# Twelve pairs of column tiles of a second block's input projection by seven block products, with the recurrence's gates and output gates laid out anew

## Chip, core and metric
One NeuronCore of one Trainium2 chip runs the whole program. The time is the device time of an execution in microseconds (us), as the median of three runs. The engines are TensorE (PE, matmuls; its weight loads are PEld), VectorE (DVE), ScalarE (ACT), GpSimd (POOL) and SyncE (SP), whose queue issues the DMAs.

## What is computed
Two transformer blocks, float32, 1024 tokens of width 1024. Block 1 is a windowed attention and a SwiGLU feed-forward; it is touched only in that its feed-forward calls a function now that held its text before. Block 2 begins with a mixer, and its input projection is what changes:

```python
proj = h @ w_in          # h: 1024 x 1024, w_in: 1024 x 5832
(q_m, k_m, v_m, o_m, i_m, f_m, c_q, c_kv, k_r, gate_pre) = jnp.split(proj, IN_SPLIT_POINTS, axis=-1)
qk = jax.nn.silu(causal_depthwise_conv(jnp.concatenate([q_m, k_m], axis=-1), conv_w, conv_b))
...
y_m = mlstm_chunkwise(q_m, k_m, v_m, log_i, log_f).reshape(B, S, M_V_WIDTH)
y_m = jax.nn.sigmoid(o_m) * y_m
...
merged = g_m * (y_m @ w_branch_m) + g_a * (y_a @ w_branch_a)
```

The widths are 1024 for q_m and k_m together, 1024 for v_m, 1024 for o_m (output gates), 4 and 4 for i_m and f_m (the recurrence's gates), 384 for c_q (query latents), 256 and 64 for c_kv and k_r (key latents), 2048 for gate_pre (gates of the merge).

## The kernel before
**Precision.** Each operand of a large product is split into a high part in a shorter float format (written by ScalarE) and a low rest (written by VectorE, high subtracted from the source). `split` does it, and `mm3` and `product` issue three matmuls for each block: high by high, low by high, high by low. `TH` and `TL` hold the split activations, transposed: 8 slices of 128 channels by 1024 tokens.

**Two forms of a projection.** `col_rows` makes a column tile: 128 output columns are the stationary weights and 512 tokens move, so a tile takes two halves of 8 x 3 = 24 matmuls, 48 in all; the result lies transposed (channels by tokens). `token_rows` makes 128 tokens by up to 512 columns: the activations are stationary and the weight columns move.

**Seven products.** The feed-forward of block 1 makes pairs of column tiles by a scheme with 7 block products in place of 8 (Strassen in Winograd's form): `block_sums` writes sums of the quarters of the activations (in place over a quarter of `TH` and `TL`, and into buffers), `left_sums` sums of the weights, which go to region 1 (`SP`). A pair takes 7 x 12 = 84 matmuls. The first pair is made in the usual way (`usual_first`, `usual_second`), because the sums are not there yet. `pair` makes the other pairs while `prep` prepares the weights of the next one.

**Order in block 2.** After the last pass of block 1 the norm of the second token half ends; meanwhile the first halves of three convolution tiles and of the recurrence's gates run on TensorE. `half_to_T` transposes the second half. Then: eight tiles of q_m and k_m (`conv`), each followed at once by its convolution on VectorE (four steps, lines 960 and 963) and a SiLU, stored in `qkd`; query latents and key latents by tokens; v_m and o_m by tokens (line 1034 onwards), o_m with the sigmoid, both stored by tokens; then the recurrence (`mlstm`, eight chunks of three steps), between whose steps the 16 tiles of the merge's gates are made as other work for TensorE; then `branch_m`, which loads the recurrence's output by tokens and transposes it into `TH` and `TL`.

**What sets the order.** The kernel is written on a tile framework. For each engine it draws up a list of instructions when the program is built: an instruction that is ready by its plan goes first if it stands earlier in the program, and one whose buffer or operand isn't ready is passed over. So the order on an engine isn't that of the source, but is fixed in the program. Buffers come from pools with a fixed number of slots per tag: `k4` 8, `vx` 4, `h2` 8, `k2` 4, `raw`, `wh`, `wl` 3 each; PSUM has three `mm`, three `s` and two `tp` banks. The big regions R1 to R3 are passed on whole: R1 is `Y`, then `SP` or `PU` (weights), then `ML` (recurrence), then `RC`.

Of the kernel before, what the change touches and what calls it, by code (L numbers as in the profile page):

```python
# [35 lines left out]
class Kernel:  # L36
# [554 lines left out]
    def block_sums(self, B):  # L591
# [23 lines left out]
        for k in range(4):  # L615
# [5 lines left out]
            nc.scalar.activation(x00, p00, AF.Identity, bias=B0)  # L621
            V.scalar_tensor_tensor(t1, p01, B0, x00, op0=OP.add, op1=OP.subtract)
# [49 lines left out]
    def block1_ffn(self, dbg=None):  # L672
# [39 lines left out]
        def first_two(j):  # L712

            A, T = self.left_parts(W[j]), self.T
            TT[j] = t = {}
            ps = self.pany()
            self.product(ps, A["a11"], T["00"])
            t[0] = self.h2([128, 512], "p1")
            nc.scalar.activation(t[0], ps, AF.Copy)
            yield  # L720
            ps = self.pany()
            self.product(ps, A["a12"], T["10"])
            t[2] = self.h2([128, 512], "sa")
            V.tensor_tensor(t[2], ps, t[0], op=OP.add)
            nc.scalar.activation(t[2], t[2], AF.Silu)

        def out(j, half, m):
            s = slice(half * 512, half * 512 + 512)
            h, l = self.h2([128, 512], "mh", F32R), self.h2([128, 512], "ml", F32R)
            self.split(h, l, m)  # L730
            for d, t in zip(midd, (h, l)):
                nc.sync.dma_start(d[j, :, s], f32(t))

        def pair(j, early):
# [21 lines left out]
            V.tensor_tensor(t[0], t[0], t[2], op=OP.mult)  # L756
            out(j, 0, t[0])
            yield
            add(t[1], t[1], "s4", "11")
            nc.scalar.activation(t[1], t[1], AF.Silu)  # L760
            V.tensor_tensor(t[3], t[3], t[1], op=OP.mult)
            out(j, 1, t[3])
            del W[j], TT[j]

# [9 lines left out]
        kept = []  # L774

        def usual_first():
            for n, A in enumerate(parts):
                ps = self.pany()
                self.product(ps, A["a11"], self.T["00"])
                p = self.h2([128, 512], "p1")  # L780
                nc.scalar.activation(p, ps, AF.Copy)
# [3 lines left out]
                t = self.h2([128, 512], "c1")  # L785
                V.tensor_tensor(t, ps, p, op=OP.add)
                kept.extend((p, t))
                if n == 0:
                    nc.scalar.activation(t, t, AF.Silu)
                    yield  # L790
            V.tensor_tensor(t, t, kept[1], op=OP.mult)
            out(0, 0, t)

        def usual_second():
            for A, p in zip(parts, (kept[0], kept[2])):
# [4 lines left out]
                if p is kept[0]:  # L800
                    nc.scalar.activation(p, p, AF.Silu)
            V.tensor_tensor(p, p, kept[0], op=OP.mult)
            out(0, 1, p)
# [7 lines left out]
        for k, _ in enumerate(self.block_sums(B2)):  # L811
            next(f, None)
        usual_second()
        SP = self.region(1, "SP", F32R)
        for _ in prep(1, True):
            pass
        cc2 = self.silu_col(a["c_2"], "cc2")
        mods = self.all_mods(("ada", self.cc, (("G2", 5, (0.0, "ffn_norm_post")),), 3, True),
                             ("mod", cc2, (("A3", 1, (1.0, "norm1_g_2")), ("B3", 0, None), ("Gm", 2, None),
                                           ("A4", 4, (1.0, "norm2_g_2"))), 3, True))  # L820
        for j in range(1, NH):
            nxt = prep(j + 1, False) if j + 1 < NH else iter(())
            for n, _ in enumerate(pair(j, j == 1)):
                next(nxt, None)
                if j > 1 and n in (0, 2, 4):
                    next(mods, None)
            for _ in nxt:
                pass
        for _ in mods:
            pass  # L830
        mods = self.all_mods(("mod", cc2, (("B4", 3, None), ("Ge", 5, None)), 3))
# [78 lines left out]
        for _ in norms:  # L910
            pass
        self.qkd = self.dram.tile([8, 128, S], F32, name="qkd")
# [33 lines left out]
    def conv(self, m):  # L946
# [3 lines left out]
        u = self.wunit(self.wcols("w_in_2", m * 128, 128), (8, 128))  # L950
        x = (self.k4 if m == 2 else self.vx)([128, S], "cx")
        for half in range(2):
            s = slice(half * 512, half * 512 + 512)
            ps = self.pany()
            self.col_rows(ps, half, u)
            nc.scalar.activation(x[:, s], ps, AF.Copy)
            if half == 0:
                yield
        o = self.k4([128, S], "co")
# [8 lines left out]
    def gates(self):  # L968

        nc, a = self.nc, self.a  # L970
        raw = self.h2([128, 8, 36], "gw")
        nc.gpsimd.memset(raw, 0.0)
        nc.sync.dma_start(raw[:, :, 0:4], self.wcols("w_in_2", 3072, 4))
        nc.sync.dma_start(raw[:, :, 32:36], self.wcols("w_in_2", 3076, 4))
        gh, gl = self.h2([128, 8, 36], "gwh", F32R), self.h2([128, 8, 36], "gwl", F32R)
        self.split(gh, gl, raw)
        gb = self.const.tile([36, 1], F32, name="gbias")
        nc.sync.dma_start(gb[0:4, :], a["igate_b_2"].rearrange("o h -> h o"))
# [10 lines left out]
    def block2_proj(self):  # L989
# [8 lines left out]
        for m in range(3, 8):  # L998
            for _ in self.convs[m]:
                pass  # L1000
# [982 lines left out]
```

## Time and profile before

| | us |
|---|---|
| median of 3 runs (lowest, highest) | 2809.21 (2807.45, 2810.56) |
| the profiled execution | 2807.71 |
| its span, first to last instruction | 2805.8 |
| TensorE busy in the span | 2627.1 |
| VectorE busy | 1765.9 |
| ScalarE busy | 1249.7 |

The mean granted clock of TensorE over the span is 0.976 of full speed. A busy TensorE is not one at its peak, because matmuls overlap; how many of them start in a stretch tells more. The change touches the stretch from 1190 to 1776 us of the span. A line like L724 is a line of the kernel's source; "out<-in" gives the tiles that an instruction writes and reads, and a note in brackets tells how long its engine was idle before it and what ended that.

### The profile page before, as it was taken

The page shows a single profiled execution, that of the slowest core. Times are in us where ns is not written, and L with a number is a line of the kernel's source. Part 1 is how long each engine was busy: PE and PEld are TensorE (multiplying, and loading weights), DVE is VectorE, ACT ScalarE, POOL GpSimd, SP SyncE. Part 2 cuts the span into 40 slices and gives each one's busy share as a digit, 9 for nine tenths or more (in the row PEclk, how much of TensorE's full clock was granted, in tenths as well). Part 3 has the DMA queues.
Part 4 walks back from the last instruction along what each step waited for, and adds up shares of the span by engine and source line. Part 5 has one row for each costly group of instructions (what it writes and reads, how often), then busy time and mean ns, then how long its engine had stood idle before and what let it go on. Part 6 is the DMA issues. An engine that isn't in the chain of part 4 may idle for free. (4 is left out here: it accounts for less than half of the span.)

```text
span 2805.8 us, 36372 instructions
## 1 busy us (share of the span) xinstructions
PE 2627.1 (94%) x13158; PEld 2116.6 (75%) x13158; DVE 1765.9 (63%) x3663; ACT 1249.7 (45%) x2183; POOL 219.3 (8%) x204
## 2 busy tenths in 40 slices
PE   6999998999999999899999999999999998889992
PEld 4766676788888787679888888788887887777771
DVE  6666549988887432866310444547777478788885
ACT  4666645333333210234222333435556444677772
POOL 0000002000000000200000000000000200343320
PEclk9999999999999999999999999999999999899996
DMA  7233113455555962534334565450111454799995
GB/s 245 91 98 98 37 75 120 130 167 168 172 170 164 292 190 83 171 104 147 118 109 128 177 172 170 152 180 14 31 31 61 152 196 164 247 341 322 314 325 177
DMA packets 316747, 442.11 MB, mean 158 GB/s; under 512 B 41633, under 2 KB 213726, under 8 KB 316566
## 3 DMA queue, kind: packets, MB, share of 16 engines
q1 hardware_dynamic: 307350, 422.97, 45.6%
q0 software_dynamic: 9216, 16.81, 2.5%
q8 instruction: 104, 1.70, 0.2%
q14 instruction: 77, 0.63, 0.1%
HBM read 354.39 MB, written 102.06 MB: 163 GB/s over the span
## 5 line engine op out<-in xcount | busy, mean ns | idle before, releaser
L164 DVE TENSOR_TENSOR wl<-raw,wh 128x1024 fp32r<-128x1024 f32 (+2 forms) x107 | 132.9, 1242 | 243.7 <-ACT wh L163 233.0
L163 ACT ACTIVATE wh<-raw 128x1024 fp32r<-128x1024 f32 (+2 forms) x107 | 111.5, 1043 | 238.2 <-PE mm L220 142.1
L164 DVE TENSOR_TENSOR mgl<-X,MH 128x1024 fp32r<-128x1024 f32 x91 | 110.0, 1221 | 16.5 <-ACT MH L163 16.0
L221 PE MATMUL mm<-TH,wl 128*128 128x512 f32 x288 | 114.6, 398 | 0.0
L219 PE MATMUL mm<-TH,wh 128*128 128x512 f32 x288 | 114.5, 397 | 0.0
L220 PE MATMUL mm<-TL,wh 128*128 128x512 f32 x288 | 114.2, 396 | 0.0
L1785 PEld LDWEIGHTS pss<-mgl,xh 128*128 128x128 f32 x512 | 96.4, 189 | 22.3
L163 ACT ACTIVATE MH<-X 128x1024 fp32r<-128x1024 f32 x91 | 96.3, 1062 | 37.8 <-DMA X<-in_w_expert_up_dram 15.9
L252 DVE SCALAR_TENSOR_TENSOR acc<-raw,cc,acc 128x1024 f32<-128x1024 f32 x70 | 89.8, 1283 | 30.9 <-DMA raw<-in_mod_w_dram 28.9
L219 PE MATMUL pss<-TH,wh 128*128 128x512 f32 x240 | 97.8, 408 | 5.7 <-ACT TH L163 4.4
L1785 PE MATMUL pss<-mgl,xh 128*128 128x256 f32 x512 | 102.9, 282 | 0.0
L1783 PE MATMUL pss<-MH,xh 128*128 128x512 f32 x256 | 102.7, 401 | 0.0
L1786 PE MATMUL pss<-MH,xl 128*128 128x512 f32 x256 | 101.6, 397 | 0.0
L442 DVE CUSTOM_DVE_ANT_0 pp<-pss,bias 128x384 f32<-128x384 f32 (+1 forms) x128 | 63.4, 521 | 54.4 <-PE pss L438 53.5
L220 PE MATMUL pss<-TL,wh 128*128 128x512 f32 x240 | 96.6, 403 | 0.0
L221 PE MATMUL pss<-TH,wl 128*128 128x512 f32 x240 | 96.3, 401 | 0.0
L551 POOL TENSOR_TENSOR Y<-Y,G 128x1024 f32<-128x1024 f32 x16 | 39.4, 2463 | 705.5 <-ACT junk L159 700.4
L228 PE MATMUL mm<-TH,wh 128*128 128x512 f32 x192 | 78.5, 410 | 1.0 <-ACT TH L350 1.0
L449 ACT ACTIVATE pp<-pp,mx 128x384 f32<-128x384 f32 (+1 forms) x128 | 73.8, 579 | 11.6 <-DVE mx L445 11.6
L229 PE MATMUL mm<-TL,wh 128*128 128x512 f32 x192 | 77.6, 404 | 0.0
L230 PE MATMUL mm<-TH,wl 128*128 128x512 f32 x192 | 76.6, 399 | 0.0
L219 PE MATMUL mm<-WD,mTh 128*128 128x512 f32 x128 | 55.6, 435 | 22.3 <-ACT mTh L163 22.3
(744 smaller groups left out, 8127.0 us busy)
## 6 DMA issues: line engine op xcount, KB each, us to landing
raw<-in_mod_w_dram SPq DMA_DIRECT2D x48, 512.0 KB
X<-in_w_expert_gate_dram SPq DMA_DIRECT2D x47, 512.0 KB
X<-in_w_expert_down_dram SPq DMA_DIRECT2D x47, 512.0 KB
raw<-in_ffn_w_in_dram SPq DMA_DIRECT2D x45, 512.0 KB
X<-in_w_expert_up_dram SPq DMA_DIRECT2D x44, 512.0 KB
raw<-in_w_in_dram SPq DMA_DIRECT2D x40, 512.0 KB
raw<-in_ada_w_dram SPq DMA_DIRECT2D x32, 512.0 KB
midh<-mh SPq DMA_DIRECT2D x44, 256.0 KB
```

Of the source, the lines that this page charges most:

```text
L163: self.nc.scalar.activation(h, src, AF.Copy)
L164: (engine or self.nc.vector).tensor_tensor(l, src, f32(h), op=OP.subtract)
L219: nc.tensor.matmul(ps, ah, bh, start=i == 0, stop=False)
L220: nc.tensor.matmul(ps, ah, bl, start=False, stop=False)
L221: nc.tensor.matmul(ps, al, bh, start=False, stop=i == n - 1)
L228: nc.tensor.matmul(ps, ah, bh, start=i == 0, stop=False)
L229: nc.tensor.matmul(ps, ah, bl, start=False, stop=False)
L230: nc.tensor.matmul(ps, al, bh, start=False, stop=i == n - 1)
L252: nc.vector.scalar_tensor_tensor(acc, raw, cc[:, k:k + 1], acc, op0=OP.mult, op1=OP.add)
L1783: nc.tensor.matmul(ps, xh[:, k], gh, start=k == 0, stop=False)
L1785: nc.tensor.matmul(ps[:, c], xh[:, k], self.ML[n + c][:, m], start=False, stop=False)
L1786: nc.tensor.matmul(ps, xl[:, k], gh, start=False, stop=k == 7)
```

## The change
The scheme of seven products becomes a function, `seven`, that the feed-forward of block 1 and now the projection of block 2 call. In block 2 it makes 24 column tiles, in 12 pairs: the 8 of q_m and k_m, the 8 of o_m and the last 8 of the merge's gates. The results are stored as they are (`qkr`, `og`, `gd`). Since the sums overwrite a quarter of `TH` and `TL`, `block_sums` also writes that quarter unsplit (`x01`) and stores it, and it is loaded and split again after the last pair.

After the pairs come the key latents by tokens, with the eight columns of the recurrence's gates beside them (356 columns with zeros between); the gates are transposed after each tile. Then the eight convolutions, whose input is loaded from `qkr`; then v_m by tokens. The query latents move into the recurrence as work between its first eight steps, and the first eight tiles of the merge's gates stay between the other sixteen. In `mlstm` the output gates are no longer loaded and multiplied; ScalarE scales the output. In `branch_m` each transposed group of 512 tokens is multiplied by the sigmoid of the loaded output gate before it is split.

```diff
-    def block_sums(self, B):
+    def block_sums(self, B, kept=None):
...
             nc.scalar.activation(x00, p00, AF.Identity, bias=B0)
+            if kept is not None:
+                x01 = self.k2([128, 512], "x01")
+                nc.scalar.activation(x01, p01, AF.Identity, bias=B0)
+                nc.sync.dma_start(kept[k], x01)
...
+    def seven(self, n, src, B, norms, done, after, beside, kept=None):
...
+        f = usual_first()
+        for _ in norms:
+            next(f, None)
+        for _ in f:
+            pass
+        f = first_two(1)
+        for _ in self.block_sums(B, kept):
+            next(f, None)
+        usual_second()
+        SP = self.region(1, "SP", F32R)
+        for _ in prep(1, True):
+            pass
+        after()
+        for j in range(1, n):
+            nxt = prep(j + 1, False) if j + 1 < n else iter(())
+            for m, _ in enumerate(pair(j, j == 1)):
+                next(nxt, None)
+                beside(j, m)
+            for _ in nxt:
+                pass
...
-        self.convs = [self.conv(m) for m in range(8)]
-        first = self.convs[0:3] + [self.gates()]
-        for u in first:
-            next(u)
-        self.half_to_T(1, B3)
-        for u in first:
-            next(u, None)
+        self.norms2, self.B3 = norms, B3
...
-        u = self.wunit(self.wcols("w_in_2", m * 128, 128), (8, 128))
...
-            self.col_rows(ps, half, u)
-            nc.scalar.activation(x[:, s], ps, AF.Copy)
...
+        x, o = self.k4([128, S], "cx"), self.k4([128, S], "co")
+        nc.sync.dma_start(x, self.qkr[m])
...
+        tiles = [(m * 128, self.qkr[m]) for m in range(8)] + [(2048 + m * 128, self.og[m]) for m in range(8)]
+        tiles += [(3784 + m * 128, self.gd[m]) for m in range(8, 16)]
+
+        def done(j, c, half, t, first):
+            nc.sync.dma_start(tiles[2 * j + c][1][:, half * 512:half * 512 + 512], t)
+
+        self.seven(12, lambda j: [self.wcols(W, c0, 128) for c0, _ in tiles[2 * j:2 * j + 2]], self.B3, self.norms2, done,
+                   lambda: None, lambda j, n: None, x01d)
+        for k in range(4):
+            t = self.h2([128, 512], "x01")
+            nc.sync.dma_start(t, x01d[k])
+            self.split(self.TH[:, k, 512:1024], self.TL[:, k, 512:1024], t)
...
+            for c0, n, at in ((3464, 320, 0), (3072, 4, 320), (3076, 4, 352)):
+                nc.sync.dma_start(raw[:, :, at:at + n],
+                                  a[W][0, u * 256:u * 256 + 256, c0:c0 + n].rearrange("(k p) m -> p k m", p=128))
...
+            pt, s = self.ptp((36, 128)), slice(i * 128, i * 128 + 128)
+            nc.tensor.transpose(pt, gt, self.ident)
+            nc.scalar.activation(self.LI[:, s], pt[0:4], AF.Identity, bias=gb[0:4])
+            nc.scalar.activation(self.FG[:, s], pt[32:36], AF.Identity, bias=gb[32:36])
+        for m in range(8):
+            self.conv(m)
...
-        for c0, dst, f in ((1024, self.vd, AF.Copy), (2048, self.od, AF.Sigmoid)):
...
+        for nh in range(2):
+            units = self.kunits(W, 1024 + nh * 512, 512, 2, 3, PU if nh else None)
...
-            nc.sync.dma_start(og, self.od[s, :])
...
-                V.scalar_tensor_tensor(y[:, h * 256:h * 256 + 256], pn[:, 0:256], rd, og[:, h * 256:h * 256 + 256],
-                                       op0=OP.mult, op1=OP.mult)
+                nc.scalar.activation(y[:, h * 256:h * 256 + 256], pn[:, 0:256], AF.Copy, scale=rd)
...
-        for m in range(16):
...
+        for i in range(NT):
+            next(step)
+            ps = self.pany((128, 384))
+            self.token_rows(ps, i, units)
...
+        for m in range(8):
...
-                if (m % 2, half) != (1, 1):
-                    next(step)
+                next(step)
...
-                self.split(TH[:, k, s], TL[:, k, s], ps)
+                g = self.h2([128, 512], "og")
+                nc.sync.dma_start(g, self.og[k, :, s])
+                nc.scalar.activation(g, g, AF.Sigmoid)
+                nc.vector.tensor_tensor(g, ps, g, op=OP.mult)
+                self.split(TH[:, k, s], TL[:, k, s], g)
```

The parts of `seven` that are left out (`prep`, `first_two`, `pair`, `usual_first`, `usual_second`) are those of the feed-forward before, with the product of the two tiles and the SiLU taken out into `done`.

## Rows read from the trace of the kernel before
**Rows 1.** page, part 1: engine, busy us, share of the span, instructions
```profile
PE 2627.1 (94%) x13158; PEld 2116.6 (75%) x13158; DVE 1765.9 (63%) x3663; ACT 1249.7 (45%) x2183; POOL 219.3 (8%) x204
```

**Rows 2.** stretches (us): busy us by engine (instructions), granted clock, DMA share, GB/s
```profile
481.15:510.60 29.45, 23.70 (x111) 18.39 (x109) 29.17 (x45) 18.93 (x30) 0.00 (x0) 0.88 0.06 19
510.60:921.00 410.40, 409.25 (x1789) 328.80 (x1789) 334.92 (x446) 141.23 (x190) 0.34 (x1) 1.00 0.55 173
...
1206.90:1212.40 5.50, 5.50 (x25) 2.70 (x24) 0.00 (x0) 0.60 (x1) 0.00 (x0) 1.00 0.00 0
1212.40:1222.30 9.90, 8.60 (x53) 6.56 (x52) 5.04 (x7) 6.57 (x10) 0.00 (x0) 1.00 0.00 0
...
1364.00:1534.90 170.90, 170.90 (x753) 139.47 (x753) 15.46 (x17) 33.01 (x46) 2.79 (x8) 1.00 0.35 107
1534.90:1756.30 221.40, 221.40 (x1132) 186.58 (x1131) 99.15 (x231) 73.08 (x119) 8.26 (x14) 1.00 0.58 176
```

**Rows 3.** timeline of ScalarE (start, length, line): two evictions of first halves
```profile
1268.39 0.60 ACT L956 ACTIVATE cx<-pss 128x512 f32<-128x512 f32 x1 [4.24 <-PE pss L221]
...
1279.59 0.60 ACT L956 ACTIVATE cx<-pss 128x512 f32<-128x512 f32 x1 [4.29 <-PE pss L221]
```

**Rows 4.** the adds of line 724: count, min/median/max ns, first and last start
```profile
L724 DVE TENSOR_TENSOR sa<-pss,p x11: 683/685/691, 533.1 to 904.3; 128x512 f32<-128x512 f32 x11
L724 DVE TENSOR_TENSOR sa<-mm,p x10: 682/684/696, 493.8 to 868.1; 128x512 f32<-128x512 f32 x10
```

**Rows 5.** timeline of TensorE: first products of two pairs of latent tiles
```profile
1329.49 0.31 PE L219 MATMUL pss<-wh,TH 128*128 128x320 f32 x1
...
1336.53 0.31 PE L219 MATMUL pss<-wh,TH 128*128 128x320 f32 x1
```

**Rows 6.** timeline of TensorE in block 1's block sums; idle in brackets
```profile
490.84 0.77 PE L609 MATMUL pt<-ident,Y 128*128 128x128 f32 x4 [2.37 <-ACT x L621]
...
492.05 0.63 PE L220 MATMUL pss<-TL,wh 128*128 128x512 f32 x1
492.48 0.63 PE L221 MATMUL pss<-TH,wl 128*128 128x512 f32 x1
...
501.62 0.79 PE L219 MATMUL pss<-TH,wh 128*128 128x512 f32 x1 [3.37 <-ACT TH L163]
```

**Rows 7.** timeline of VectorE: the last write of the second norm
```profile
1204.68 1.28 DVE L559 SCALAR_TENSOR_TENSOR Y<-xt,rs,A 128x1024 f32<-128x1024 f32 x1
```

**Rows 8.** timeline of VectorE: convolution steps, a later low half, two ropes
```profile
1226.34 0.81 DVE L960 TENSOR_SCALAR co<-cx,cw,cvb 128x1024 f32<-128x1024 f32 x1
...
1231.05 0.81 DVE L960 TENSOR_SCALAR co<-cx,cw,cvb 128x1024 f32<-128x1024 f32 x1
...
1254.48 1.28 DVE L963 SCALAR_TENSOR_TENSOR co<-cx,cw,co 128x1021 f32<-128x1021 f32 x1
1255.68 0.95 DVE L164 TENSOR_TENSOR PU<-raw,PU 128x768 fp32r<-128x768 f32 x1
...
1339.58 0.19 DVE L1048 TENSOR_TENSOR kr<-kr,cs 128x32 f32<-128x32 f32 x1 [0.72 <-ACT kr L1022]
...
1342.70 0.19 DVE L1048 TENSOR_TENSOR kr<-kr,cs 128x32 f32<-128x32 f32 x1 [0.71 <-ACT kr L1022]
```

**Rows 9.** timeline of VectorE: one chunk of the recurrence
```profile
1690.02 0.48 DVE L1170 SCALAR_TENSOR_TENSOR C<-C,ML,pss 128x258 f32<-128x258 f32 x1 [4.56 <-PE pss L221]
...
1693.88 1.23 DVE L164 TENSOR_TENSOR Cl<-C,Ch 128x1032 fp32r<-128x1032 f32 x1
...
1703.16 1.23 DVE L164 TENSOR_TENSOR wl<-raw,wh 128x1024 fp32r<-128x1024 f32 x1 [8.05 <-ACT wh L163]
...
1713.01 0.48 DVE L1159 SCALAR_TENSOR_TENSOR ML<-pss,rd,ML 128x256 f32<-128x256 f32 x1
```

**Rows 10.** timeline of VectorE: low halves behind the output transposes
```profile
1760.54 1.37 DVE L164 TENSOR_TENSOR TL<-pt,TH 128x512 fp32r<-128x512 f32 x2 [0.78 <-ACT TH L163]
1762.62 1.37 DVE L164 TENSOR_TENSOR TL<-pt,TH 128x512 fp32r<-128x512 f32 x2 [0.70 <-ACT TH L163]
```

More of the change, by code (lines that the diff above doesn't have):

```diff
@@ L696, in block1_ffn @@
         src = lambda j: [w_in[0, :, c:c + 128].rearrange("(k p) m -> p k m", p=128) for c in (j * 128, (NH + j) * 128)]
-        W, TT = {}, {}
-        def upper(j, raw):
-            W[j] = [self.wp.tile([128, 1024], F32R, name=n, bufs=self.hl_bufs) for n in ("wh", "wl")]
-            self.split(W[j][0], W[j][1], raw)
-        def prep(j, lone):
-            raw = [self.raw_unit(u, (8, 128)) for u in src(j)]
-            if not lone:
-                upper(j, raw[0])
-            yield
-            W[j] += [self.k2([128, 512], n, F32R) for n in ("a22h", "a22l")] + [SP[:, j % 2 * 4 + n] for n in range(4)]
-            yield from self.left_sums(raw, W[j][2:4], W[j][4:])
@@ L727, in out @@
-        def out(j, half, m):
+        def done(j, c, half, t, first):
+            if c == 0:
+                nc.scalar.activation(t, t, AF.Silu)
+                return
+            V.tensor_tensor(t, t, first, op=OP.mult)
             s = slice(half * 512, half * 512 + 512)
             h, l = self.h2([128, 512], "mh", F32R), self.h2([128, 512], "ml", F32R)
-            self.split(h, l, m)
+            self.split(h, l, t)
             for d, t in zip(midd, (h, l)):
                 nc.sync.dma_start(d[j, :, s], f32(t))
-        def pair(j, early):
-            A, T = self.left_parts(W[j]), self.T
-            for _ in () if early else first_two(j):
-                yield
-            t = TT[j]
-            def add(dst, src, *ab):
-                ps = self.pany()
-                self.product(ps, A[ab[0]], T[ab[1]])
-                V.tensor_tensor(dst, ps, src, op=OP.add)
-                return ps
-            yield
-            add(t[0], t[0], "s2", "t2")
-            yield
-            t[1], t[3] = self.h2([128, 512], "u4"), self.h2([128, 512], "c22")
-            ps = add(t[1], t[0], "s1", "t1")
-            yield
-            add(t[0], t[0], "s3", "t3")
-            V.tensor_tensor(t[3], ps, t[0], op=OP.add)
-            yield
-            add(t[0], t[0], "a22", "t4")
[L756 to L763, printed above, removed]
@@ L766, in block1_ffn @@
-        C = []
-        for u in src(0):
-            C += [self.wp.tile([128, 1024], F32R, name=n, bufs=self.hl_bufs) for n in ("wh", "wl")]
-            self.split(C[-2], C[-1], self.raw_unit(u, (8, 128)))
-        upper(1, self.raw_unit(src(1)[0], (8, 128)))
-        self.T = {"00": ([TH[:, k, 0:512] for k in range(4)], [TL[:, k, 0:512] for k in range(4)]),
-                  "10": ([TH[:, 4 + k, 0:512] for k in range(4)], [TL[:, 4 + k, 0:512] for k in range(4)])}
-        parts = [self.left_parts(C[0:2]), self.left_parts(C[2:4])]
@@ L774, in block1_ffn @@
[L774 to L781, printed above, removed]
-                yield
-                ps = self.pany()
-                self.product(ps, A["a12"], self.T["10"])
[L785 to L792, printed above, removed]
@@ L794, in usual_second @@
-        def usual_second():
-            for A, p in zip(parts, (kept[0], kept[2])):
-                ps = self.pany()
-                self.mm3(ps, [(A[x][0][k], A[x][1][k], self.T[y][0][k], self.T[y][1][k])
-                              for x, y in (("a11", "t1"), ("a12", "11")) for k in range(4)])
-                V.tensor_tensor(p, ps, p, op=OP.add)
[L800 to L803, printed above, removed]
@@ L805, in block1_ffn @@
-        f = usual_first()
-        for _ in norms:
-            next(f, None)
-        for _ in f:
-            pass
-        f = first_two(1)
[L811 to L831, printed above, removed]
+        late = {}
+        def after():
+            cc2 = late["cc2"] = self.silu_col(a["c_2"], "cc2")
+            late["mods"] = self.all_mods(("ada", self.cc, (("G2", 5, (0.0, "ffn_norm_post")),), 3, True),
+                                         ("mod", cc2, (("A3", 1, (1.0, "norm1_g_2")), ("B3", 0, None), ("Gm", 2, None),
+                                                       ("A4", 4, (1.0, "norm2_g_2"))), 3, True))
@@ L834, in block1_ffn, with beside @@
+        def beside(j, n):
+            if j > 1 and n in (0, 2, 4):
+                next(late["mods"], None)
+        self.seven(NH, src, B2, norms, done, after, beside)
+        for _ in late["mods"]:
+            pass
+        mods = self.all_mods(("mod", late["cc2"], (("B4", 3, None), ("Ge", 5, None)), 3))
         wide = lambda f: [f([128, 1024], n, F32R) for n in ("oh", "ol")]
@@ L966, in conv @@
         nc.sync.dma_start(self.qkd[m], o)
[L968 to L978, printed above, removed]
-        nc.sync.dma_start(gb[32:36, :], a["fgate_b_2"].rearrange("o h -> h o"))
-        self.LI, self.FG = self.k4([4, S], "LI"), self.k4([4, S], "FG")
-        for half in range(2):
-            s = slice(half * 512, half * 512 + 512)
-            ps = self.pany()
-            self.col_rows(ps[0:36], half, (gh, gl))
-            nc.scalar.activation(self.LI[:, s], ps[0:4], AF.Identity, bias=gb[0:4])
-            nc.scalar.activation(self.FG[:, s], ps[32:36], AF.Identity, bias=gb[32:36])
-            yield
     def block2_proj(self):
```

165 lines of the change are left out of this document (118 added, 47 removed).

## The prediction
> **What bounds the kernel now.** I read the engines' shares first, then the stretches around the change, then single lines of the timeline. TensorE (PE) is busy 94% of the span [rows 1]. Then the table of stretches. In the part that the change touches, from the first convolution product at 1190.1 us to the last gate tile at 1756.3, it is bound by TensorE almost alone: the stretches from 1364 to 1534.9 and from 1534.9 to 1756.3 have no idle PE at all, while VectorE (DVE) is busy 15 of 171 and 99 of 221 us [rows 2]. Its only gap here is 1.3 us, in the transposes of the second token half from 1212.4 to 1222.3 [rows 2]. So a matmul that goes is worth its time, as long as nothing else then makes TensorE wait; the question is what waits come in.
>
> **Part 1, 24 column tiles.** A usual column tile takes 48 matmuls. The first halves of two neighbouring tiles are evicted at 1268.39 and 1279.59, so a tile takes 11.20 us and a pair 22.40 [rows 3]. The same pair by seven block products runs in block 1 already, 84 matmuls: its second add comes 20 times between 533.1 and 904.3 us, which is 371.2 / 19 = 19.54 us a pair [rows 4]. The stretch of these pairs has 409.25 of 410.40 us PE busy [rows 2], with more DVE work than the new pairs have (they store their results as they are, without the product, the SiLU and the split). Eleven of the twelve pairs go this way: 11 x (22.40 - 19.54) = **31.5 us off**. That is 0.2333 us a matmul for the usual tile. One correction: eight of the 24 tiles, the output gates, were made by tokens before, and there 753 matmuls take 170.9 us, 0.227 each [rows 2]; 384 x 0.006 = 2.3, and as records can be missing I take **2.0 us back**.
>
> **Part 2, what the scheme costs at its start.** The block sums need the second token half of Y. Until then the new kernel has 72 matmuls to do (four products of the first pair, two of the second), as many as the three convolution halves that fill 1190.1 to 1206.9 before. That cover ends at 1206.9. The last norm write ends at 1204.68 + 1.28 = 1205.96 [rows 7]; two more adds of 0.69 [rows 4] in DVE's queue make it 1207.4, so the cover is about long enough. Then comes the stage itself, and block 1 shows it whole: from the first sum at 481.15 to the first product that needs a weight sum at 510.60, 29.45 us, of which DVE is busy 29.17 [rows 2]. It is DVE-bound, so TensorE's waits in it (2.37 and 3.37 us) cannot be filled, and after each one the clock is at its lower level: 0.43 us from matmul to matmul where 0.233 is usual [rows 6]. In block 1 part of it was covered by two products that block 2 has done by then, but since DVE sets its length I take the same 29.45. The stage then ends at 1207.4 + 29.45 = 1236.9, with 120 matmuls of projection done, worth 120 x 0.2333 = 28.0 us. So of 46.8 us 18.8 are lost. Before, the same place lost the 32 transposes and the gap: 53 matmuls in 8.60 us of PE, of which 21 products x 0.233 = 4.9, leaves 3.7, and 1.3 idle: 5.0 [rows 2]. Net **13.8 us back**, between 11 (the clock does not fall) and 20 (the copy of x01, kept and stored, uses the last of four 512-wide buffers in each round and delays the next).
>
> **Part 3, the gates of the recurrence.** Their own products go: 2 x 5.50 us, since a product of 36 columns of weights takes as long as any other [rows 2]: **11.0 off**. As 36 more moving columns of the latents' key product they cost less: two such tiles of 320 columns start 7.04 us apart, 0.1467 us a matmul [rows 5], so 356 columns cost some 0.1467 x 356/320 = 0.163; 192 x 0.0165 = **3.2 back**. Eight small transposes: four take 0.77 at the low clock [rows 6], so at most 1.5, I take **0.9 back**.
>
> Sum on TensorE: -31.5 + 2.0 + 13.8 - 11.0 + 3.2 + 0.9 = **-22.6 us**. The query latents and half of the merge gates change places and the output-gate tiles are in part 1; they cost TensorE the same elsewhere.
>
> **Part 4, waits that are not in the trace of before.**
> (a) Key latents after the last pair. Their weights go into the region that the pairs' weight sums hold until the last product; then ScalarE copies, DVE subtracts (0.95 [rows 8]), and DVE may be inside a 1.28 us convolution step: 1.8 to 6 us, I take **3** (nearest to copy plus subtraction plus one step).
> (b) The convolutions. Before, each was spread beside 11 us of products. Now all eight stand between the latents and the value projection, their input reloaded from DRAM, so nothing on TensorE hides inside them: 4.71 us each on DVE (1226.34 to 1231.05 [rows 8]), 37.7 in all. The latents' chains share DVE: from one rope to the next 3.12 us with 0.71 idle, 2.4 x 8 = 19. TensorE's cover there is 192 x 0.163 = 31 us. The value weights' low halves are queued behind. If they come in between the steps, the price is 0; if strictly behind, 28 (below). The trace shows the former: at 1255.68 the low half of a later weight sits between two steps of one convolution, and again after the next [rows 8]; each step must wait for the one before it, and something else is put into the gap. The order is a list made by readiness, not by the program's lines. I take **4**.
> (c) The recurrence beside less work. Its eight chunks share 221.4 us with 32 gate halves of 24 x 0.2333 = 5.6 [rows 2], which leaves 5.3 of its own PE work a chunk. Three steps make a chunk; beside query tiles (0.1467 x 384/320 x 24 = 4.2 each [rows 5]) it has 5.3 + 12.6 = 18 us, beside gate halves 22. Its own chain is shorter: from the state's update at 1690.02 to the end of its split at 1695.1 it takes 5 us, from 1704.4 to the last output at 1713.5 another 9, and in between DVE idles 8.05 us waiting for a gate tile's weight [rows 9]. With the update's own products 15 to 16, so 0 to 5, I take **1**. The output scaling moves to ScalarE, which is busy 73 of 221 us [rows 2]: nothing.
> (d) Applying the output gates after the transposes. 16 groups get one more DVE multiply of 0.69, as the add from PSUM in [rows 4]. Two groups now take 1.37 us of DVE in 2.08 [rows 10]; with two multiplies 2.7, so DVE becomes the limit: 8 x 0.62 = 5.0. The sigmoids can run ahead, and later latents' transposes fill in: 0 to 11 (16 x 0.69, nothing hidden), I take **4**.
> (e) DMA, all on SP's queue, which works in order: 16 more stores of 256 KB, eight loads of 512 KB for the convolutions, four stores and loads of x01, and eight loads of gates by tokens become 16 by columns. That is about 10 MB more over some 250 us, 40 GB/s on stretches that move 107 and 176 GB/s at shares of 0.35 and 0.58 [rows 2]: hidden; 0, and at most the 3 us of a load that comes late behind a waiting store.
> Together 12 us. Net -10.6.
>
> **Forecast.** The profiled execution took 2807.7 us (span 2805.8, 1.9 around it), so 2797.1 on its scale; the median of the three runs is 1.5 above it: **2799 us** (2798.6), -0.4%. Runs of this kernel can tell about 0.2%, 5.6 us, from no change: below 2803.6 is faster, above 2814.8 slower. With the bounds (sums 11 to 20, (a) 1.8 to 6, (b) 0 to 8, (c) 0 to 5, (d) 0 to 8) the forecast's own range is 2787 to 2803: 0.48.
>
> **Rivals.**
> *Value weights behind the convolutions, slower.* Two convolutions in flight fill each other's gaps, and then a weight half finds none. DVE has 4 x 0.95 + 19 + 37.7 + 1.2 = 62 us in front of the first usable value weight, less about 3 before the last product; TensorE has 34 of its own. Stall 25, plus 1.8 of low clock after it (0.12 x 29.45 us were lost with two such waits [rows 2]), less the 4 counted: +23, **2822**. It decides from a stall of 20 us on. For it: 37.7 of DVE work in one place, where DVE was the idle engine. Against: the interleaving in [rows 8]. 0.14.
> *The covers cost about twice what I take* (sums 20, (b) 10, (d) 8): +15, **2811**, no change. For it: four waits priced from neighbours. 0.24.
> *The recurrence is no longer covered.* If a chunk took 25 us, its chain would end 8 x 4 = 32 us late, **2830**. Against: the 8 us idle in each chunk. 0.04.
> *The clock stays low through the sums.* In block 1 it comes back to the full level within the stage, at 0.88 over the whole; at 1212.4 transposes mixed with products ran at 1.00 [rows 2]. At the low level all 48 products of the second half of the first pair would take 48 x 0.2 = 9.6 more, of which the 11 us of waiting in the stage take most: +3, **2802**, 0.05, inside the range. The Trainium skill (TensorE: Matmul & The Clock Gate, "Part 4: PE-mode transpose") says that the full clock does not engage for transposes, which would be the mechanism; the row of 1212.4 does not agree with it as far as a mixture goes.
> *The four waits come out free:* -22.6, **2787**, 0.05; less than that only if the sums are shorter too, since the pairs cannot give more than 31.5.
>
> **Chances.** Faster: 0.48 + 0.05 (free) + 0.03 of the clock's 0.05 = 0.56. Same: the other 0.02 and 0.24 = 0.26. Slower: 0.14 + 0.04 = 0.18. Range: 2786 to 2820, from the free end to just under the first slower rival; outside lie some 0.09 of that, the 0.04 and 0.03 of the free end, 0.16.
>
> **What would show it.** Pairs of about 19.5 us between adds of the projection; a stretch of some 29 us with DVE full before them and PE near 0.6 busy; no gate products of 36 weight columns; after the last pair a gap of PE of a few us, then key latents, then value products with no gap over 8 us. If PE is idle 20 us before the first value product, with convolution steps on DVE, the slower rival holds. If PE idles within the recurrence's chunks, the third. Wrong in the gain itself it would be if a pair took over 20.5 us (DVE or the stores as the limit).

## The result and the profile after

| | before | changed |
|---|---|---|
| median (lowest, highest), us | 2808.46 (2807.24, 2812.23) | 2823.98 (2818.80, 2828.59) |
| ratio to before, 95% interval | | 1.0052 [1.0039, 1.0065] |
| profiled execution / span, us | 2807.71 / 2805.8 | 2824.64 / 2822.9 |

The change makes the kernel slower by 0.5%, some 15 us. The forecast was 2799 and the range ended at 2820.

First the page of the changed kernel, the TensorE line; [rows 1] is the one of before. There are 140 matmuls fewer, but the span is 17.1 us longer, so time was lost in waiting.

```profile
PE 2615.4 (93%) x13018; PEld 2107.2 (75%) x13018; DVE 1884.3 (67%) x3826; ACT 1283.1 (45%) x2258; POOL 221.2 (8%) x207
```

Then its stretches (columns as in [rows 2]): the pairs from the first product of a weight sum to the last; the latents' end with the first value products; the other value products; the recurrence's first chunk, its query tiles, its gate tiles.

```profile
1241.60:1449.70 208.10, 208.10 (x901) 168.80 (x899) 119.66 (x158) 43.80 (x52) 0.44 (x3) 1.00 0.38 114
...
1484.60:1525.00 40.40, 29.61 (x109) 22.31 (x108) 36.32 (x83) 19.41 (x43) 1.54 (x5) 0.87 0.75 265
1525.00:1589.50 64.50, 64.50 (x284) 52.64 (x282) 19.39 (x18) 18.99 (x24) 2.00 (x3) 1.00 0.32 112
1589.50:1606.00 16.50, 9.63 (x64) 9.00 (x64) 4.16 (x14) 3.69 (x9) 1.26 (x1) 0.81 0.78 174
1606.00:1653.50 47.50, 44.85 (x279) 44.23 (x279) 28.95 (x119) 24.91 (x56) 4.33 (x13) 0.96 0.58 170
1653.50:1769.50 116.00, 116.00 (x612) 98.57 (x611) 59.18 (x134) 56.13 (x95) 5.94 (x8) 1.00 0.64 194
```

The pairs and the last two thirds of the recurrence are full, as [rows 2] had it for the old forms. Two places aren't, the rows of 40.40 and 16.50 us. From 1484.6 to 1525.0 only 109 matmuls start in 40.4 us, while the next 64.5 us hold 284; at that pace the 109 need 24.8 us, so 15.6 us are lost, and the granted clock is 0.87. From 1589.5 to 1606.0 TensorE is busy 9.6 of 16.5 us, at 0.81.

The timeline of TensorE names what ended each wait (in brackets: idle us, what ended it):

```profile
1450.63 0.43 PE L219 MATMUL mm<-PU,TH 128*128 128x356 f32 x1 [0.93 <-ACT PU L163]
...
1496.53 0.29 PE L1024 MATMUL pt<-ident,gates 128*36 128x128 f32 x1 [3.32 <-ACT gates L1020]
...
1507.86 0.40 PE L1024 MATMUL pt<-ident,gates 128*36 128x128 f32 x1 [5.31 <-ACT gates L1020]
...
1516.95 0.50 PE L220 MATMUL mm<-ul,TH 128*128 128x512 f32 x1 [2.16 <-DVE ul L164]
...
1603.48 1.65 PE L1135 MATMUL pt<-ML 128*128 128x128 f32 x6 [6.69 <-DVE SD L1137]
...
1646.19 0.44 PE L219 MATMUL pss<-wh,TH 128*128 128x384 f32 x1 [2.47 <-ACT cq L1193]
```

By stretch, from the start of one kind of instruction on TensorE to the next (before: 566.2 us from the first projection product to the first output transpose, 1049.5 us behind it):

| us | usual tiles and sums | pairs | latents, values | recurrence | rest |
|---|---|---|---|---|---|
| forecast | 46.8 | 209.4 | 123.4, and 3 ahead | 166.4 | 1053.5 |
| changed | 49.0 | 208.1 | 139.9, and 0.9 ahead | 178.8 | 1053.5 |

The forecast's row is put together from its terms: values 384 x 0.227 = 87.2, latents 31.3 + 0.9, wait (b) 4; recurrence 221.4 - 16 x 5.6 + 8 x 4.2 + 1; the rest is 1049.5 + (d) 4. (The row adds up to 13.2 us less than before, the forecast's net is 10.6; the stretches of before hold a little more than its terms.) 28.9 us too much stand in two columns. Two things scatter from run to run, so that no effect of the change is read from them: the first projection product starts between 1189.9 and 1196.1 us (1190.1 before, 1192.6 here), and the last column takes 1049.9 to 1057.6 us in the runs with this kernel's 13018 matmuls. So its 1053.5, exactly the forecast's, is luck.

**The latents and values.** Timeline of VectorE, the norm of one latent tile (L105 to L124) with convolution steps (L961, L964) between its own:

```profile
1485.02 0.15 DVE L105 TENSOR_SCALAR ms<-ss 128x1 f32<-128x1 f32 x1
...
1486.41 0.14 DVE L107 TENSOR_SCALAR rs<-ms 128x1 int32<-128x1 int32 x1
1486.48 0.81 DVE L961 TENSOR_SCALAR co<-cx,cw,cvb 128x1024 f32<-128x1024 f32 x1
1487.20 0.21 DVE L113 SCALAR_TENSOR_TENSOR rt<-rs,ms 128x1 f32<-128x1 f32 x1
1487.33 1.28 DVE L964 SCALAR_TENSOR_TENSOR co<-cx,cw,co 128x1021 f32<-128x1021 f32 x1
...
1493.62 1.27 DVE L964 SCALAR_TENSOR_TENSOR co<-cx,cw,co 128x1021 f32<-128x1021 f32 x1
1494.81 0.15 DVE L124 TENSOR_TENSOR rs<-rs,rt 128x1 f32<-128x1 f32 x1
```

and what ScalarE then does for that tile: scale it, then copy its gates, for which the transpose at 1496.53 above waited:

```profile
1495.80 0.47 ACT L1016 ACTIVATE ck<-mm,rs 128x256 f32<-128x256 f32 x1
...
1496.27 0.20 ACT L1020 ACTIVATE gates<-mm 128x36 f32<-128x36 f32 x1
```

Each small step of the norm is followed by a long one of something else. The chain takes 9.9 us from 1485.02 to 1494.96. In the kernel before, the same nine steps of a latent tile take 1.8 us:

```profile
1340.19 0.15 DVE L105 TENSOR_SCALAR ms<-ss 128x1 f32<-128x1 f32 x1
...
1341.83 0.16 DVE L124 TENSOR_TENSOR rs<-rs,rt 128x1 f32<-128x1 f32 x1
```

**The first chunk.** The last product that reads region 1, the loads into it (SyncE's queue), and GpSimd's first use of the broadcast rows:

```profile
1589.15 0.39 PE L221 MATMUL pss<-PU,TL 128*128 128x512 f32 x1
...
1589.57 0.37 SPq L1121 DMA_DIRECT2D ML<-qkd  x1
...
1590.63 0.42 SPq L1122 DMA_DIRECT2D ML<-rr  x1
...
1600.08 1.26 POOL L1130 TENSOR_TENSOR Dm<-ML,causal 128x512 f32<-128x512 f32 x1 [61.01 <-DMA ML<-rr]
```

Region 1 holds the second half of the value weights, so the first chunk's queries, keys and rows are requested when the last value product has run, and the rows arrive 9.5 us later. GpSimd's sum with them, exponentials on ScalarE and a product on VectorE (1602.74) must follow before TensorE's transposes at 1603.48, the ones with the wait of 6.69 us. Before, the first half of each width had the region, and the same rows were loaded beside products, and first used 34 us ahead of the recurrence's first transposes (1535.22):

```profile
1490.64 0.42 SPq L1120 DMA_DIRECT2D ML<-rr  x1
...
1500.78 1.30 POOL L1128 TENSOR_TENSOR Dm<-ML,causal 128x512 f32<-128x512 f32 x1 [178.65 <-DMA ML<-rr]
```

### The profile page after: what moved, and what is told of

It reads as the page before. It is cut to its first block, busy times and chain, and to the rows that moved or that the text cites. A ratio compares the mean times of both kernels' runs of the same rounds, so it can differ in the third digit from the quotient of the medians.

```text
span 2822.9 us, 36499 instructions
## 1 busy us (share of the span) xinstructions
PE 2615.4 (93%) x13018; PEld 2107.2 (75%) x13018; DVE 1884.3 (67%) x3826; ACT 1283.1 (45%) x2258; POOL 221.2 (8%) x207
## 3 DMA queue, kind: packets, MB, share of 16 engines
q1 hardware_dynamic: 320406, 433.98, 46.8%
## 5 line engine op out<-in xcount | busy, mean ns | idle before, releaser
L163 ACT ACTIVATE wh<-raw 128x1024 fp32r<-128x1024 f32 (+1 forms) x101 | 104.6, 1039 | 185.6 <-DMA raw<-in_ffn_w_in_dram 44.5
L164 DVE TENSOR_TENSOR wl<-raw,wh 128x1024 fp32r<-128x1024 f32 (+1 forms) x101 | 126.0, 1250 | 69.3 <-ACT wh L163 67.1
L1805 PEld LDWEIGHTS pss<-mgl,xh 128*128 128x128 f32 x512 | 96.9, 189 | 22.6
L163 ACT ACTIVATE SP<-raw 128x1024 fp32r<-128x1024 f32 x64 | 67.8, 1060 | 78.7 <-DVE raw L648 43.3
L164 DVE TENSOR_TENSOR SP<-raw,SP 128x1024 fp32r<-128x1024 f32 x64 | 78.0, 1220 | 13.2 <-ACT SP L163 13.2
L219 PE MATMUL pss<-TH,wh 128*128 128x512 f32 x176 | 74.5, 423 | 7.0 <-ACT TH L163 6.9
L228 PE MATMUL mm<-TH,wh 128*128 128x512 f32 x192 | 78.5, 410 | 1.0 <-ACT TH L350 1.0
L229 PE MATMUL mm<-TL,wh 128*128 128x512 f32 x192 | 77.5, 404 | 0.0
L230 PE MATMUL mm<-TH,wl 128*128 128x512 f32 x192 | 76.7, 399 | 0.0
L221 PE MATMUL pss<-TH,wl 128*128 128x512 f32 x176 | 73.1, 415 | 0.0
L164 DVE TENSOR_TENSOR WD<-X,WD 128x1024 fp32r<-128x1024 f32 x47 | 56.9, 1223 | 21.4 <-ACT WD L163 19.2
```

The lines of the kernel that those rows point to most:

```text
L163: self.nc.scalar.activation(h, src, AF.Copy)
L164: (engine or self.nc.vector).tensor_tensor(l, src, f32(h), op=OP.subtract)
L219: nc.tensor.matmul(ps, ah, bh, start=i == 0, stop=False)
L228: nc.tensor.matmul(ps, ah, bh, start=i == 0, stop=False)
L229: nc.tensor.matmul(ps, ah, bl, start=False, stop=False)
L230: nc.tensor.matmul(ps, al, bh, start=False, stop=i == n - 1)
```

## The experiments

Each run is compared with the kernel before on the same chip; the stretches are as in the table above.

### Convolutions left out

```diff
-        nc.vector.tensor_scalar(o, x, cw[:, 24 + m:25 + m], cbias[:, m:m + 1], op0=OP.mult, op1=OP.add)
-        for j in range(3):
...
-        nc.scalar.activation(o, o, AF.Silu)
+        nc.scalar.activation(o, x, AF.Silu)
```

> The changed kernel without the four convolution steps of each of the eight convolutions (the loaded rows go straight into the SiLU, so 37.7 us of VectorE work are left out of the computation; loads, SiLU and stores stay). Theory A: convolution steps slip between the nine dependent steps of each latent tile's norm, so that its chain takes some 11 us and the gate transposes behind it hold up TensorE: the 40.4 us after the last latent product, with 109 matmuls, shrink by some 13 us; about 2811 us, ratio to the kernel before 1.001, and no wait over 1 us in front of a gate transpose. Rival B: TensorE is held there by the place of the transposes and of the weights' copies on ScalarE, whatever VectorE does: 2822 to 2824, ratio 1.005, and waits of 3 and 5 us still in front of the transposes.

2808.50 us, 0.9998 [0.9988, 1.0007]. Latents and values take 124.9 us, 15.0 less than in the changed kernel; the recurrence stays long, at 176.9. So the convolutions' work on VectorE makes the first loss. That it is their place and not their amount, the next run tells.

### Convolutions behind the values

```diff
-        x, o = self.k4([128, S], "cx"), self.k4([128, S], "co")
+        x, o = self.wp.tile([128, S], F32, name="cx", tag="raw", bufs=self.raw_bufs), self.k4([128, S], "co")
...
-        for m in range(8):
-            self.conv(m)
...
+        for m in range(8):
+            self.conv(m)
```

(the loop moves behind that of the values)

> All eight convolutions are done, but emitted behind the value projection, their input in the ring of raw weights, so that they start when the value weights have been split. Theory A: VectorE does the same work, but not between the steps of the latents' norms: about 2812 us, ratio 1.0015, like the kernel without convolutions. Rival B (the place of the transposes): 2824, ratio 1.005. Rival C: the sheer 37.7 us of VectorE work cost it, wherever they stand before the recurrence: 2820 or more, the first chunk or the gate rows late.

2808.93 us, 0.9995 [0.9985, 1.0004]: the whole gain, with all the work done. Latents and values take 125.8 us, with the clock at full level and no wait over 0.6 us:

```profile
1451.10:1576.90 125.80, 123.36 (x600) 103.87 (x600) 85.01 (x170) 61.58 (x110) 5.72 (x9) 1.00 0.60 203
1576.90:1756.10 179.20, 169.52 (x934) 150.89 (x933) 92.51 (x265) 83.94 (x158) 11.34 (x22) 0.97 0.64 187
```

The recurrence remains at 179.2 us. Rival C, the amount, is out.

### Gates ahead of the norm

The four lines that evict and transpose the gates move from behind the scaling to behind the products.

> The gates of each latent tile are evicted and transposed at once, ahead of the tile's norm, not behind its scaling; the convolutions stay where they are. Theory A1: TensorE only waits because the transposes stand behind the norm's chain: the waits of 3.3 and 5.3 us and the low clock after them go, some 9 us less, 2815 us, ratio 1.002. Theory A2: the chain also holds PSUM banks, so the wait moves to the value products: at most 3 us less, 2821 to 2824.

2822.06 us, 1.0041 [1.0026, 1.0056], 139.4 us for latents and values. Theory A2: no transpose waits any more, but products wait in their place, for ScalarE's last copy out of a latent tile's PSUM bank (line 1024 is that copy here):

```profile
1496.77 0.80 PE L219 MATMUL pss<-wh,TH 128*128 128x512 f32 x1 [6.11 <-ACT kr L1024]
...
1508.06 0.80 PE L219 MATMUL mm<-wh,TH 128*128 128x512 f32 x1 [3.69 <-ACT kr L1024]
```

So the transposes are only the first to meet the long chain. It holds the gates and the bank alike.

### Own buffers for the first chunk

```diff
+        own = [self.vx([128, 8, 128], n) for n in ("qk0", "bc0")]
         C = self.vx([128, 4, 258], "C")
...
+            if c == 0:
+                qk, bc = own
```

> The first chunk's queries and keys and its broadcast rows get buffers of their own, so that they no longer wait for region 1, which holds the second half of the value weights until their last product. Theory D: the 6.7 us of idle TensorE in the first chunk and the low clock behind it come from these loads, issued at 1589.6 when the last value product reads the region and landed at 1600: about 9 us less, 2815 us, ratio 1.002. Rival E: the chain of the first chunk itself (exponentials, product, splits) is longer than one query tile covers: at most 2 us less, 2822.

2817.84 us, 1.0029 [1.0018, 1.0039]. The 6.7 us wait is gone and the recurrence takes 171.3 us, 7.5 less; four waits of 0.8 to 2.2 us remain in it. Theory D, with some 6 us in the total where 9 were expected. The second chunk's rows still wait for the region: they are used at 1598.97, when the recurrence has begun.

### The first half of the value weights in region 1

```diff
-            units = self.kunits(W, 1024 + nh * 512, 512, 2, 3, PU if nh else None)
+            units = self.kunits(W, 1024 + nh * 512, 512, 2, 3, None if nh else PU)
```

> The changed kernel with the first, not the second, half of the value weights in region 1, so that the region is free for the recurrence some 43 us before the last value product. Theory D (the region's handover delays the first chunk's loads): the 6.7 us wait in the first chunk goes, 6.5 us less as with buffers of its own, but the first value weights now wait for the last latent product, 3 us more: 2818 to 2821 us, and the first chunk's rows land before the last value product. Rival E2 (the loads are late because of the order of the DMA queue, not the region): the rows still land after 1595, 2824.

2811.28 us, 1.0006 [0.9996, 1.0016]: 13 us less than the changed kernel, where 3 to 6 were expected. The recurrence takes 165.9 us where the forecast has 166.4, at full clock; three of the four waits that own buffers left don't occur, and the second chunk's rows are used at 1568.28, 30 us before the first query product. Latents and values take 143.9, because value weights' low halves now stand between convolution steps, and TensorE waits for them:

```profile
1495.96 0.79 PE L220 MATMUL mm<-PU,TH 128*128 128x512 f32 x1 [6.50 <-DVE PU L164]
...
1508.74 0.79 PE L220 MATMUL mm<-PU,TH 128*128 128x512 f32 x1 [5.68 <-DVE PU L164]
...
1598.00:1763.90 165.90, 163.85 (x924) 146.24 (x923) 92.61 (x265) 83.49 (x159) 8.73 (x14) 1.00 0.61 188
```

This is the mechanism of the forecast's slower rival, with 12.2 of its 25 us, in the one layout where it occurs.

### Four buffers for the broadcast rows

```diff
-            bc, y = R[:, b + 2].rearrange("p (m t) -> p m t", m=8), R[:, b + 3]
+            bc, y = R[:, b + 1 + c // 2 % 2].rearrange("p (m t) -> p m t", m=8), R[:, b + 3]
```

> The changed kernel with the recurrence's broadcast rows in four buffers, not two. Theory F: beside query tiles a chunk is so short (18 us) that the rows of a later chunk, loaded when a buffer is freed at 1632 and landed at 1641.8, come too late for its exponentials, and ScalarE then holds the query tile's bank: the wait of 2.5 us and the low clock behind it go, 3 us less, 2820 us, ratio 1.004. Rival G: the wait is for ScalarE's own queue, and stays: 2823, ratio 1.005.

2826.22 us, 1.0056 [1.0041, 1.0070]; no gain. The fourth chunk's wait of 2.5 us is gone, so theory F names it rightly, but the recurrence takes 185.5 us, with a new wait of 5.8:

```profile
1600.64 6.22 SPq L1122 DMA_DIRECT2D ML<-rr  x2
...
1612.12 4.02 SPq L1127 DMA_DIRECT2D v<-vd  x2
...
1626.07 1.06 ACT L163 ACTIVATE vh<-v 128x1032 fp32r<-128x1032 f32 x1 [8.76 <-DMA v<-vd]
...
1629.78 0.58 PE L219 MATMUL mm<-vh,SDp 128*128 128x258 f32 x1 [5.80 <-ACT SDp L163]
```

Five broadcasts now go out after the handover of the region, from 1591.08 to 1611.68; the value load behind them, requested at 1612.12, is used at 1626.07, 14 us later (in the changed kernel 5.7), and the second chunk's products wait.

### Three edits together

> Three edits together: the convolutions behind the value projection, the first chunk's loads in buffers of their own, and the broadcast rows of the recurrence in four buffers of the region, not two. If the stalls are separate, they add up: 15.5 and 6.5 us less than the changed kernel, and some 3 for the fourth chunk: 2799 to 2802 us, ratio to the kernel before 0.997. Rival: moved behind the value projection the convolutions end so late that the first chunk's loads wait for their results, and the second edit gains nothing: 2808, ratio 0.9995.

2807.74 us, 0.9992 [0.9984, 1.0001]: no more than the late convolutions alone. The first chunk's wait is gone, but a wait of 6.0 us stands where the run before had its 5.8, and the recurrence takes 176.4:

```profile
1610.95 0.58 PE L219 MATMUL mm<-vh,SDp 128*128 128x258 f32 x1 [6.04 <-ACT SDp L163]
```

### Two edits together, without the four buffers

> Convolutions behind the value projection and buffers of its own for the first chunk, without the four row buffers. If the new 6 us wait in the run with all three edits comes from the four row buffers (their broadcasts stand before the value loads in the DMA queue), it is gone: 2802 us, ratio 0.9975. Rival: it comes from the two other edits together (results of late convolutions): 2807, ratio 0.999, with the 6 us wait in place.

2802.69 us, 0.9970 [0.9959, 0.9981]: late convolutions and own buffers add up (126.9 and 170.4 us), and the 6 us wait isn't there. It came from the four buffers.

### Late convolutions, first half in region 1

> Convolutions behind the value projection and the first half of the value weights in region 1. In the runs before, the second of these alone brought the recurrence down to 166 us from its first query tile to its end, as the forecast's sum has it, but paid 13.9 us of waits for value weights, whose low halves stood between convolution steps. If the convolutions are out of the way, the two gains add up: 13 us less than with the convolutions moved alone, and up to 3 us back for the weights behind the last latent product: 2796 to 2800 us, ratio to the kernel before 0.996. Rival: the waits for the value weights come from region 1 itself, which holds the latents' weights until their last product, and stay without the convolutions: 2806 to 2809, ratio 0.999.

2800.13 us, 0.9965 [0.9951, 0.9978], faster than both kernels, with the forecast's time. The stretches of latents and values and of the recurrence:

```profile
1452.00:1580.80 128.80, 124.79 (x611) 105.18 (x612) 85.42 (x170) 58.79 (x109) 11.58 (x17) 1.00 0.68 216
1580.80:1748.90 168.10, 165.73 (x924) 148.17 (x923) 92.36 (x265) 84.06 (x159) 8.59 (x14) 0.99 0.63 185
```

128.8 and 168.0 us, 21.9 less than changed. The waits for value weights shrink to one of 1.4 us; the region itself makes no more than that, and the rest came from the convolutions. In this run a latent tile's norm runs from 1490.25 to 1492.05, 1.8 us, where it took 9.9:

```profile
1490.25 0.14 DVE L105 TENSOR_SCALAR ms<-ss 128x1 f32<-128x1 f32 x1
...
1491.89 0.16 DVE L124 TENSOR_TENSOR rs<-rs,rt 128x1 f32<-128x1 f32 x1
```

### The same with four row buffers

> Convolutions behind the value projection, the first half of the value weights in region 1, and four buffers for the recurrence's broadcast rows. If the 6 us wait that the four buffers brought before came from five broadcasts at the moment when the region was handed over, with the value loads of the second chunk behind them, it isn't here, because the region is free some 25 us before the recurrence starts, and the wait of 2.4 us for the rows of the fourth chunk goes too: 2796 to 2798 us, ratio to the kernel before 0.9955. Rival: more rows ahead always push the value loads back: the 6 us wait comes again, 2804 to 2806, ratio 0.998.

2802.33 us, 0.9965 [0.9952, 0.9979]. Neither: the 6 us wait doesn't come and the 2.4 us of the fourth chunk go, but two waits of 2.5 and 0.6 us come in the first chunk, for a query weight. Its load, behind five broadcasts, is requested at 1575.91 and used at 1584.13, 8.2 us later; in the run before, behind three, it took 4.6:

```profile
1585.03 0.44 PE L219 MATMUL mm<-uh,TH 128*128 128x384 f32 x1 [2.45 <-ACT uh L163]
1586.02 0.69 PE L220 MATMUL mm<-ul,TH 128*128 128x384 f32 x1 [0.55 <-DVE ul L164]
```

The recurrence takes 168.7 us, as without. In these runs rows ahead of time cost whoever is behind them in the queue.

### No kept quarter

`block_sums` gets no `kept`, and the loop that loads and splits it goes.

> The changed kernel without the kept quarter: it is not written, stored, loaded and split again (so that the latents and values are computed from a sum in its place, and what follows has other data; only the stretch up to the values is read). By the forecast's upper bound the copies lengthen the block sums: 29.5 us from the first sum to the first product of a weight sum, not 30.7, and so 1 to 2 us less up to the latents. Rival: they cost nothing there, and the stage is 30.7 us as before.

2822.51 us in one run. First sum and first product of a weight sum, of the changed kernel and of this run:

```profile
1210.92 0.75 DVE L626 SCALAR_TENSOR_TENSOR t<-pt,B,x 128x512 f32<-128x512 f32 x1 [1.21 <-ACT x L624]
...
1241.57 0.39 PE L672 MATMUL mm<-TH,SP 128*128 128x512 f32 x1
```

```profile
1210.13 0.75 DVE L626 SCALAR_TENSOR_TENSOR t<-pt,B,x 128x512 f32<-128x512 f32 x1 [0.49 <-PE pss L609]
...
1239.53 0.39 PE L672 MATMUL mm<-TH,SP 128*128 128x512 f32 x1
```

30.65 against 29.40 us, and the first sum no longer waits 1.2 us for the copy of the kept quarter, only 0.5 for its transposes. The copies cost 2.0 us in the first column of the table (47.0 for 49.0).

### No multiply by the output gates

> The changed kernel without the multiply by the output gates behind the transposes (16 operations of 0.69 us on VectorE left out of the computation; the gates' loads and sigmoids stay). The forecast's term (d), VectorE as the limit of this stretch: 4 to 5 us less, 2818 us, ratio 1.0035. Rival H: the loads of the gates or ScalarE's sigmoids set the pace of the stretch: 0 to 1 us less, 2822.

2839.40 us, 1.0105 [1.0090, 1.0120], and it can't be read from this: the kernel leaves out the gates, so the experts at the end of the program are chosen from other numbers, and their loop runs over as many blocks as there are; TensorE has 13072 matmuls in place of 13018, and the rest takes 1069.8 us in place of 1053.5. (The runs without convolutions and without the kept quarter have 13018.) In its own stretch, from the first output transpose to the last, it takes 18.8 us, the changed kernel 20.7, the kernel before 16.8. So of the 3.9 us lost there about half is the multiply, between what the two theories say; the other runs with the multiply take 19.9 to 21.1, and what makes the other half isn't shown. VectorE in the changed kernel, low halves and multiplies back to back:

```profile
1775.61 1.89 DVE L164 TENSOR_TENSOR TL<-og,TH 128x512 fp32r<-128x512 f32 x3
1777.41 1.28 DVE L1224 TENSOR_TENSOR og<-pt,og 128x512 f32<-128x512 f32 x2
```

## Why the prediction was wrong, point by point

**The pairs** came as forecast: 901 matmuls in 208.1 us with TensorE full [rows 2, 4]; 209.4 was the sum.

**The block sums**: 29.45 us were taken and 30.65 measured; with a first sum 1.0 us later it makes 2.2 (16.0 net for the 13.8 taken, on the way to the bound of 20, for which the copy of the kept quarter was the reason given). The run without the copy has the 29.4 of [rows 2]. The rival of the low clock doesn't hold: transposes mixed with products run at a granted clock of 1.00, the upper level; in this stage it falls to 0.50, the lower, only behind waits (below, behind one of 3.50 us), and comes back within the stage:

```profile
1207.10:1217.90 10.80, 10.32 (x64) 8.33 (x63) 9.24 (x19) 7.27 (x13) 0.00 (x0) 1.00 0.19 72
...
1231.40:1237.40 6.00, 6.00 (x13) 4.46 (x14) 5.68 (x10) 2.42 (x4) 0.00 (x0) 0.50 0.00 0
```

The Trainium skill (TensorE: Matmul & The Clock Gate, "Part 4: PE-mode transpose") says that the full clock does not engage for transposes. The first of these rows does not agree with it, as far as a mixture shows it.

**(a)** was 0.9 us, below the bound of 1.8.

**(b) is the first step that failed.** The forecast saw in [rows 8] that something else is put into the gaps of a chain on VectorE, and read it as cover for the value weights; its price of 0 to 28 us asked only whether these come in time. In the changed kernel they nearly do (the last one costs 2.2 us). But the latents' norms are chains on the same engine, of nine steps, and a step of up to 1.3 us in each gap makes 1.8 us into 9.9. The forecast had even counted the latents' chains, as 2.4 us a tile of VectorE's time, and not asked what waits for them: the transposes of the gates in TensorE's fixed order, and the banks. The convolutions cost 14 to 15 us in place of 4, shown by the runs with them out and moved. These still take 124.9 and 125.8 us, where the row without (b) has 119.4; small waits before the gates' transposes and 16 small transposes just before the recurrence (1.1 us) are in the difference, which no run takes apart.

**(c) is the second.** The forecast counted the recurrence's chain on VectorE, and that was right: with the loads on time three runs take 165.9 to 168.7 us, where the sum gave 166.4. It didn't follow who holds region 1. The diff turns `PU if nh == 0` into `PU if nh`, so that the region is handed over at the last value product and not half a width earlier, and the first chunk's loads, above all a broadcast of 9.5 us, come to stand on the path: some 11 to 13 us, where 1 was taken and 5 the bound. Buffers of its own for the first chunk give back 7.5 of them; the rest goes only when the later loads into the region come early too.

**(d)**: 4 taken, 3.9 measured up to the last output transpose; about half of it the multiply, so the size came out right and the reason only in part. **(e)**: no wait of TensorE ends with one of the stores and loads that the change adds; VectorE waits 0.4 us for a convolution's input in the chain shown above (at 1491.50).

**Readings.** The row of 753 matmuls [rows 2] holds 12 small transposes beside 740 products, which alone take some 0.230 us each, not 0.227; the 2.0 us back of part 1 are then 1.3. And the forecast's own range, 2787 to 2803, is narrower than its bounds added up, which give 2786 to 2820.

**The rivals.** The slower one gave 2822, near the time, but not its mechanism: before the first value product there is no wait at all, and 12.4 of the 28.9 us are in the recurrence. It occurs in the run with the first half in region 1. The recurrence is late, yet not by a chain of 25 us a chunk. With both steps mended the time is 2800, 10 us less than the kernel before on its chip (0.9965), where the forecast's net was 10.6. So the sum of the other terms holds; one by one they agree less well, as latents and values still take 128.8 us for 123.4 and the last column 1050.3 for 1053.5.

## What to carry to other kernels

Work put beside a chain on the same engine costs instead of being covered if the chain is what others wait for: count the links, and add the longest neighbour to each. When a buffer or a region changes hands in a diff, look for its next owner, and put the latency of that owner's loads on the path unless something runs in between. The 22.6 us that the forecast gains on TensorE were given back in two places, 57 us long together, in which TensorE starts few matmuls.

## What the runs showed of the hardware

A load of 512 KB that broadcasts eight rows to 128 partitions took 9.5 us from request to first use in the changed kernel and 10.1 in the one before, each time with another load requested 1 us ahead of it. What is queued behind several of them is late: 14 us for a value load behind five, 5.7 for the same load in the changed kernel. More buffers for such rows took away the wait for them in three kernels, and in each another load's wait came in its place. Nine steps of 0.15 to 0.22 us that depend on one another took 1.8 us on VectorE alone and 9.9 us with other work of 0.8 to 1.3 us between them.
